# The cross-attention query projection of a hybrid decoder block, as a streamed Strassen step in place of dense 128x512 blocks

## The chip, the core and the metric

The kernel runs on one core of one Trainium2 chip, as one launch. The metric is the device time of the launch in microseconds (us), lower is better. Before the change three timed runs gave 1946.44, 1946.65 and 1947.6 us, a median of 1946.65 us.

## The reference

One decoder layer over 1024 tokens of width 1024 in float32: a mixer (an SSD branch and a gated-linear-attention branch, merged through gates), cross-attention over 256 memory tokens, and a SwiGLU feed-forward part, each behind an RMSNorm and with a residual add. What the change touches:

```python
merged = sigmoid(g_ssd) * (y_ssd @ w_up_ssd) + sigmoid(g_gla) * (y_gla @ w_up_gla)
h = h + merged @ w_o                                   # mixer's residual
n = rmsnorm(h, norm_xattn)
q = (n @ w_xq).reshape(B, S, 4, 256)                   # <- the query projection
k, v = split(rmsnorm(mem, norm_mem) @ w_xkv, 2)
p = softmax(einsum('bshd,bmhd->bhsm', q, k) * 256 ** -0.5)
h = h + einsum('bhsm,bmhd->bshd', p, v).reshape(B, S, D) @ w_xo
h = h + (silu(g) * u) @ w_ffn_out                      # g, u = split(rmsnorm(h, norm_ffn) @ w_ffn_in, 2)
```

## The kernel before

Activations lie with channels on the 128 partitions and 1024 tokens along the row. A float32 product is made of three products of rounded halves (type fp32r): a tile is split into a high part (ScalarE, `ACT`, a copy to fp32r) and a low part (VectorE, `DVE`, a subtraction), and TensorE (`PE`) adds high x high, high x low and low x high in PSUM. `split` (L226) issues such a pair.

The large projections use a Strassen scheme in Winograd's form: seven products of quarter matrices in place of eight, called B11, B21, T1, B22, T2, T3, T4 here, with sums of quarters prepared beforehand. Five projections do not: `dense` (L1236) runs `w_up_ssd`, `w_up_gla`, `w_o`, `w_xq` and `w_xo` as 16 blocks each (8 groups of 128 output channels by 2 halves of the tokens), 24 matmuls of 128x512 a block. The text calls the first three of them dense stages 0 to 2, `w_xq` the query stage. `Left` (L1190) streams their weights: 1 MB pieces `raw` (four buffers, `aux`), split into a ring of two tiles `wd`.

Dense stage 2 (`w_o`) ends each block in `residual` (L1357): DVE adds the block to a piece `ga` of the residual stream, the sum is stored (`h_d<-ga`), `put_xq` (L1365) makes the high and low parts of the query stage's input (`hl`), and `Stats.take` (L487) squares it on ACT into one buffer `sq` and adds that to `ssum`. Which of DVE and POOL adds is decided when the program is built, by `either` (L85).

Beside the dense stages runs `presum` (L1297): for each of 11 pieces of `w_ffn_out` it loads 1 MB into the one buffer `pre`, makes four sums on POOL (one into `sa`, three in place), and stores each of them (`down_d<-sa`, `down_d<-pre`). The next load waits until the stores have read the buffer. These sums are left operands of the last Strassen products, far behind. All transfers named here are issued by SP, in the order that a scheduler wrote when the program was built: every engine takes its instructions in order, and one that waits holds up those behind it.

`load_kv` (L1385) fetches one head's keys and values into two `ga` buffers and splits them into `kvhl`. The program calls it for the first head behind the query stage, but the scheduler may write it earlier. Then attention runs per head and half of the tokens (`Att`): scores, softmax, transposes, values; the blocks of `w_xo` (dense stage 4) are written between and behind them, and the feed-forward part follows.

SBUF is shared out in slots of 8 KB a partition: 14 `op`, 4 `aux`, 4 `m`. PSUM has 8 banks: 4 `acc`, 4 `bank`.

Of the kernel before, what the change touches and what calls it, by code (L numbers as in the profile page):

```python
# [27 lines left out]
KP = D_FF // 256  # L28
# [50 lines left out]
def block_kernel(ctx: ExitStack, tc: tile.TileContext, t: dict, out: bass.AP):  # L79
    nc = tc.nc  # L80
    now = [0.0]
    PE, ACT, SP = Tensor(nc.tensor, now), nc.scalar, nc.sync
    DVE, POOL = Meter(nc.vector, now, 0.06, 1.04e-3), Meter(nc.gpsimd, now, 0.08, 2.25e-3)
# [15 lines left out]
    def dram(name, *shape):  # L99
        return dr.tile(list(shape), F32, name=name, tag=name)  # L100
# [14 lines left out]
    yg_d = dram("yg_d", D, TOK)  # L115
    act_d = dram("act_d", 7 * D_FF // 2, HALF)
    down_d = dram("down_d", 4 * D_FF // 2, HALF)
    kT_d = dram("kT_d", D, MEM)
    vm_d = dram("vm_d", MEM, D)
    cs_d = dram("cs_d", P, P)  # L120
# [105 lines left out]
    def split(src, hi, lo, e=None):  # L226
        ACT.activation(hi, src, AF.Copy)  # L227
        sub(e or DVE, lo, src, hi)
# [5 lines left out]
    class Operands:  # L234
# [44 lines left out]
    class Unit:  # L279
# [267 lines left out]
    for k in range(NB):  # L547
        p = bank()
# [633 lines left out]
    def quad(src, base, i, j):  # L1182
        q = rp.tile([P, HALF], F32, name="ga", tag="ga")
        SP.dma_start(q, src[base + i * P:base + (i + 1) * P, half(j)])
        return q

    HOME = ("aux", "aux", "m", "m")
    JS = (0, 1)

    class Left:  # L1190

        def __init__(s, mats):
            s.seq, s.raw, s.w, s.ring = [(W, u) for W in mats for u in range(4)], [], [], []

        def load(s, n):
            while len(s.raw) < min(n, len(s.seq)):
                W, u = s.seq[len(s.raw)]
                r = slot("aux", (P, NB, 256), name="raw")  # L1200
                SP.dma_start(r, W[:, 256 * u:256 * u + 256].rearrange("(k p) c -> p k c", p=P))
                s.raw.append(r)

        def upto(s, n):
            while len(s.w) < min(n, 2 * len(s.seq)):
# [12 lines left out]
            s.upto(n + 2)  # L1218
            return s.w[n]

    left = Left((t["w_up_ssd"], t["w_up_gla"], t["w_o"], t["w_xq"], t["w_xo"]))

    def paired(keys):

        return [(lambda k=k: slot(k, (P, 2, TOK), F32R, name="hl")) for k in keys]

    def hl(slots_, k):
        if callable(slots_[k]):
            slots_[k] = slots_[k]()
        return slots_[k]  # L1230

    def into(slots_, k, j, src, e=None):
        x = hl(slots_, k)
        split(src, x[:, 0, half(j)], x[:, 1, half(j)], e)

    def dense(no, ins, post, pre=lambda o, j: None, js=JS):  # L1236

        todo = [(o, j) for o in range(NB) for j in (js if o + 1 < NB else js[::-1])]
        got = [pre(*x) for x in todo[:2]]
        for n, (o, j) in enumerate(todo):  # L1240
            w = left[NB * no + o]
# [12 lines left out]

    EVEN, ODD = ("op",) * 8, ("op",) * 6 + ("aux",) * 2
    i_ys, i_yg, i_wo, i_xq, i_q, i_xo = (paired(x) for x in (EVEN, ODD, EVEN, ODD, EVEN, EVEN))

    def fetch(src, dst, gain=None):

# [34 lines left out]
    sums["m"] = pool("sa2", 2, stack=st5)  # L1294
    s1 = Stats(rp)

    def presum():  # L1297


        r = slot("m", (P, 2, D), name="pre")  # L1300
        for k in range(KP):
            SP.dma_start(r, t["w_ffn_out"][256 * k:256 * k + 256, :].rearrange("(j p) c -> p j c", p=P))
# [3 lines left out]
            put = lambda n, ap: SP.dma_start(down_d[(n * KP + k) * P:(n * KP + k + 1) * P, :], ap)  # L1306
# [12 lines left out]

    def quad_of(src):  # L1320
        return lambda o, j: quad(src, o * P, 0, j)
# [35 lines left out]
    def residual(store, stats, gain, put, scale=1.0):  # L1357
        def post(o, j, p, q):
            DVE.scalar_tensor_tensor(q, p, scale, q, ALU.mult, ALU.add)
            SP.dma_start(store[o * P:(o + 1) * P, half(j)], q)  # L1360
            put(o, j, q, col(gain, o))
            stats.take(j, q)
        return post

    def put_xq(o, j, q, g):  # L1365
        x = hl(i_xq, o)
        h, l = x[:, 0, half(j)], x[:, 1, half(j)]
        ACT.activation(h, q, AF.Copy, scale=g)
        DVE.scalar_tensor_tensor(l, q, g, h, ALU.mult, ALU.subtract)

    def waiting(g, n):
        for _ in range(n):
            yield
        for _ in g:
            yield
# [6 lines left out]

    kv = []

    def load_kv(h):  # L1385
        es = [rp.tile([P, 2, 256], F32, name="ga", tag="ga") for _ in range(2)]
        h_ = slot("m" if h < 3 else "op", (P, 2, 4, 256), F32R, name="kvhl")
        SP.dma_start(es[0], kT_d[h * 256:(h + 1) * 256, :].rearrange("(i p) m -> p i m", p=P))
        SP.dma_start(es[1], vm_d[:, h * 256:(h + 1) * 256].rearrange("(i p) c -> p i c", p=P))
        for i in range(2):  # L1390
            split(es[i], h_[:, 0, 2 * i:2 * i + 2], h_[:, 1, 2 * i:2 * i + 2])
        kv.append(h_)

    xsc = cp.tile([P, NCH], F32, name="xsc")
# [12 lines left out]
    run(dense(3, i_xq, lambda o, j, p, g: into(i_q, o, j, p)), (xq_side(), 1.0), (early, 1.0))  # L1407
    drain(early)
    load_kv(0)
    u_xo_stats = Stats(rp)  # L1410

    class Att:
# [121 lines left out]
        ACT.activation(b_xo[o][:, half(j)], q, AF.Copy, scale=g)  # L1534

    B = Operands(b_xo, 4, order=("B11", "T1", "B21", "B22", "T2", "T3", "T4"))
    for n, _ in enumerate(dense(4, i_xo, residual(h2_d, u_xo_stats, "norm_ffn", put_xo), quad_of(h1_d), js=(1, 0))):
        if n >= 8:
            B.upto(n - 7)
        if n == 12:  # L1540
            gu[0][0].load()
        if n == 14:
            gu[0][1].load()
# [207 lines left out]
```

## Time and profile before

| what | us |
|---|---|
| median of three timed runs (1946.44 to 1947.6) | 1946.65 |
| the profiled execution: its span | 1949.0 |
| PE busy in it | 1916.2 |
| DVE, ACT, POOL busy | 1298.5, 845.8, 557.8 |
| mean granted TensorE clock | 0.998 |

The profiled execution has no time of its own beside its span; the span lies 2.35 us above the median. Times in the trace count from the span's start. In a line, `acc<-hl,wd` means that a tile `acc` is written from tiles `hl` and `wd`; `x16` counts instructions; what stands behind `<-` in brackets ended the idle time before it. A matmul row's duration reaches past the start of the next, so that rates are read from starts.

### The profile page before, as it was taken

How to read it: one execution, taken by the hardware profiler on the slowest of the kernel's cores; microseconds unless marked ns; L12 is line 12 of the kernel's file. 1: busy time of each engine (PE TensorE's matmuls, PEld its weight loads, DVE VectorE, ACT ScalarE, POOL GpSimd, SP SyncE). 2: the span in 40 equal slices, each digit the busy share in tenths (PEclk: the TensorE clock that was granted, in tenths of full speed). 3: DMA queues.
4: the chain of work that ended last, by engine and by line, in shares of the span. 5: the costliest groups of instructions: out<-in, count | busy, mean ns of one | idle time of the engine just before them, and what ended most of it. 6: DMA issues, size and time to landing. Idle time of an engine off the chain costs nothing.

```text
span 1949.0 us, 26264 instructions
## 1 busy us (share of the span) xinstructions
PE 1916.2 (98%) x9776; PEld 1615.6 (83%) x9776; DVE 1298.5 (67%) x1873; ACT 845.8 (43%) x1485; POOL 557.8 (29%) x428
## 2 busy tenths in 40 slices
PE   7999999999999999999999999999999999999998
PEld 7998787888878888788887888888888888888888
DVE  7766879877776764655534237677777777766566
ACT  7534564655553444643223235444333333345243
POOL 0012334345543231022433000006445544320002
PEclk9999999999999999999999999999999999999999
DMA  9423383446553653997675201442233224177463
GB/s 341 144 93 101 130 307 107 152 161 186 174 173 123 198 167 124 348 346 270 226 269 164 82 22 44 140 141 82 90 126 110 82 100 144 42 271 239 157 224 126
DMA packets 237875, 317.98 MB, mean 163 GB/s; under 512 B 16538, under 2 KB 156036, under 8 KB 237748
## 3 DMA queue, kind: packets, MB, share of 16 engines
q1 hardware_dynamic: 236020, 310.01, 47.4%
q10 hardware_dynamic: 1728, 6.29, 0.8%
q8 instruction: 77, 1.26, 0.3%
q14 instruction: 50, 0.41, 0.1%
HBM read 215.27 MB, written 100.99 MB: 162 GB/s over the span
## 4 chain that ended last, share of the span: by engine, by line
PE 43%; DMA 3%; POOL 2%; DVE 1%; issue 1%; ACT 1%; POOLq 0%; SPq 0%; DVEq 0%; ACTq 0%
PE acc L51 38%; PE bank L51 4%; DMA pre<-in_w_ffn_out_dram 1%; POOL pre L73 1%; DMA down_d<-pre 1%; PE bank L55 1%; POOL ssum L73 0%; DVE hl L73 0%; POOL sa L73 0%; DMA h_d<-ga 0%; DMA ga<-vm_d 0%; DVE wd L73 0%; ACT wd L227 0%; ACT sq L493 0%; DVE phl L73 0%
## 5 line engine op out<-in xcount | busy, mean ns | idle before, releaser
L51 PE MATMUL acc<-hl,wd 128*128 128x512 f32 x1920 | 440.4, 390 | 3.6 <-DVE wd L73 2.0
L51 PEld LDWEIGHTS acc<-hl,wd 128*128 128x128 f32 x1920 | 359.6, 188 | 80.7 <-DVE wd L73 3.3
L73 DVE TENSOR_TENSOR wlo<-raw,whi 128x512 fp32r<-128x512 f32 x272 | 236.4, 875 | 103.6 <-ACT whi L227 103.5
L227 ACT ACTIVATE whi<-raw 128x512 fp32r<-128x512 f32 x272 | 169.5, 629 | 247.6 <-PE acc L51 201.0
L73 DVE TENSOR_TENSOR o<-acc,o 128x512 f32<-128x512 f32 (+1 forms) x256 | 172.6, 676 | 108.8 <-PE acc L51 95.4
L51 PE MATMUL acc<-fs 128*128 128x512 f32 (+1 forms) x792 | 155.7, 356 | 0.1
L51 PEld LDWEIGHTS acc<-fs 128*128 128x128 f32 x792 | 130.7, 189 | 20.8 <-issue 0.5
L73 DVE TENSOR_TENSOR fs<-fr,fs 128x1024 fp32r<-128x1024 f32 (+1 forms) x84 | 98.9, 1217 | 36.5 <-ACT fs L227 36.4
L227 ACT ACTIVATE fs<-fr 128x1024 fp32r<-128x1024 f32 (+1 forms) x84 | 79.2, 982 | 95.9 <-PE acc L51 31.2
L73 POOL TENSOR_TENSOR raw<-raw,sa 128x512 f32<-128x512 f32 x44 | 57.1, 1297 | 207.8 <-DVE wlo L73 207.8
L73 POOL TENSOR_TENSOR sa<-raw 128x512 f32<-128x512 f32 x43 | 69.6, 1619 | 107.0 <-DMA raw<-in_w_in_dram 78.9
L227 ACT ACTIVATE whi<-sa 128x512 fp32r<-128x512 f32 x96 | 59.6, 626 | 93.7 <-PE acc L51 92.3
L73 DVE TENSOR_TENSOR wlo<-sa,whi 128x512 fp32r<-128x512 f32 x96 | 80.9, 843 | 13.7 <-ACT whi L227 12.7
L73 DVE TENSOR_TENSOR wd<-raw,wd 128x1024 fp32r<-128x1024 f32 x40 | 52.8, 1323 | 47.6 <-ACT wd L227 47.2
L73 POOL TENSOR_TENSOR rstd<-rstd,mhalf 128x4 f32<-128x4 f32 (+1 forms) x7 | 8.7, 1246 | 257.0 <-DVE rstd L73 257.0
L227 ACT ACTIVATE wd<-raw 128x1024 fp32r<-128x1024 f32 x40 | 42.2, 1057 | 90.4 <-PE acc L51 89.8
L51 PE MATMUL acc<-T4h,whi 128*128 128x512 f32 x192 | 76.3, 397 | 2.4 <-DVE o L73 2.4
L51 PE MATMUL acc<-B22h,wlo 128*128 128x512 f32 x192 | 75.7, 394 | 1.5 <-DVE wlo L73 1.5
L51 PE MATMUL acc<-T1h,whi 128*128 128x512 f32 x192 | 76.3, 397 | 0.0
L51 PE MATMUL acc<-T2h,whi 128*128 128x512 f32 x192 | 75.9, 395 | 0.0
L51 PE MATMUL acc<-T3h,whi 128*128 128x512 f32 x192 | 75.9, 395 | 0.0
L51 PE MATMUL acc<-B22h,whi 128*128 128x512 f32 x192 | 75.7, 394 | 0.0
(399 smaller groups left out, 4698.6 us busy)
## 6 DMA issues: line engine op xcount, KB each, us to landing
raw<-in_w_in_dram SPq DMA_DIRECT2D x26, 1024.0 KB, 5.9
raw<-in_w_ffn_in_dram SPq DMA_DIRECT2D x22, 1024.0 KB, 6.5
act_d<-o SPq DMA_DIRECT2D x77, 256.0 KB, 2.1
fr<-act_d SPq DMA_DIRECT2D x35, 512.0 KB, 7.9
pre<-in_w_ffn_out_dram SPq DMA_DIRECT2D x11, 1024.0 KB, 10.0
fr<-down_d SPq DMA_DIRECT2D x20, 512.0 KB, 3.9
down_d<-pre SPq DMA_DIRECT2D x33, 256.0 KB, 3.1
h_d<-ga SPq DMA_DIRECT2D x32, 256.0 KB, 3.1
```

The source lines that it names most:

```text
L51: return s.e.matmul(o, x, y, **kw)
L55: return s.e.transpose(o, x, i)
L73: return f(*a, **kw)
L227: ACT.activation(hi, src, AF.Copy)
```

## The change

The query stage leaves `dense` and becomes a class `Wide`: Strassen's seven products over all 1024 channels, each product 512 x 512 x 512, done in two steps of 24 matmuls for all four groups of 128 output rows. Its weights come as quarters of `w_xq` (B11, B21, T4) or as sums of quarters (T1, B22, T2, T3), and these sums are four new items at the front of `presum`, stored in a new DRAM buffer `xqs_d`. `put_xq` keeps its result whole in four quarter tiles `rq`; their differences and the splits into `ws` are made in the stage. The products B11, T2, T3 and T4 add up in the same four `acc` banks, T1 and B22 in four `bank` banks, B21 in four others; the parts are put together in tiles `wk` and split into the attention's operands `hl`. The first head's key/value splits are held in program order late in the stage (`kv_side`), and `w_xo`'s first two weight splits are called for at step 12 (`next_left`). `presum` is advanced faster in this stage (1.5 in place of 1.0 a step).

```diff
+    class Wide:
+        SEQ = ("B11", "T1", "B22", "T2", "B21", "T3", "T4")
+        LEFT = {"B11": (0, 0), "B21": (0, 1), "T1": 0, "B22": 3, "T2": 1, "T3": 2, "T4": (1, 1)}
+        COMB = {"T1": ((0, 0), (0, 1), (0, 0)), "T2": ((0, 0), (1, 1), (0, 0)), "T3": ((0, 1), (1, 1), (0, 1)),
+                "T4": ((1, 0), (1, 0), (0, 0))}
+        RIGHT = {"B11": (0, 0), "B22": (1, 1), "B21": (1, 0), "T1": (0, 0), "T2": (0, 0), "T3": (0, 1), "T4": (1, 0)}
+        OUT = {"B11": (0, 0), "T1": (1, 1), "B22": (0, 1), "T2": (0, 1), "B21": (0, 0), "T3": (1, 1), "T4": (1, 0)}
...
+        def load(s, n):
+            while len(s.raw) < min(n, 7):
+                src = s.LEFT[s.SEQ[len(s.raw)]]
+                if isinstance(src, tuple):
+                    i, j = src
+                    w = s.W[half(j), half(i)]
+                else:
+                    w = s.sums_d[half(src), :]
+                r = slot(s.keys[len(s.raw)], (P, 4, HALF), name="wr")
+                SP.dma_start(r, w.rearrange("(k p) c -> p k c", p=P))
+                s.raw.append(r)
...
+        def prep(s, n):
+            while len(s.ops) < min(n, 14):
+                m, kp = divmod(len(s.ops), 2)
+                s.load(m + 1)
+                name, c = s.SEQ[m], slice(2 * kp, 2 * kp + 2)
+                x = [slot("op", (P, 2, 2, HALF), F32R, name="ws") for _ in range(2)]
+                with ahead():
+                    if name in s.COMB:
+                        o, a, b = (s.quad(*ij)[:, c] for ij in s.COMB[name])
+                        sub(s.two(o), o, a, b)
+                    split(s.raw[m][:, c], x[0][:, 0], x[0][:, 1])
+                    split(s.quad(*s.RIGHT[name])[:, c], x[1][:, 0], x[1][:, 1])
+                s.ops.append(x)
+        def evac(s, name, u, p):
+            i, j = s.OUT[name]
+            o = p if name == "T4" and s.base is None else s.home(i, j)[:, u]
+            first = name in ("B11", "T1", "B22")
...
+                elif first:
+                    ACT.activation(o, p, AF.Copy)
+                elif name != "T4":
+                    add(DVE, o, p, o)
+                if not first:
+                    s.post(i, j, u, o)
+        def steps(s):
...
+                for kp in range(2):
+                    s.load(m + 3)
+                    s.prep(x + 3)
+                    w, b = s.ops[x]
+                    for u in range(4):
+                        for k in range(2):
+                            for n, (a, c) in enumerate(((0, 0), (0, 1), (1, 0))):
+                                PE.matmul(banks[u], w[:, a, k, u * P:(u + 1) * P], b[:, c, k],
...
-    left = Left((t["w_up_ssd"], t["w_up_gla"], t["w_o"], t["w_xq"], t["w_xo"]))
+    left = Left((t["w_up_ssd"], t["w_up_gla"], t["w_o"], t["w_xo"]))
...
+        todo = [(t[w].rearrange("(j k p) c -> k p j c", j=2, p=P)[k], d, 4, k) for w, d in wides for k in range(4)]
+        todo += [(t["w_ffn_out"][256 * k:256 * k + 256, :].rearrange("(j p) c -> p j c", p=P), down_d, KP, k)
+                 for k in range(KP)]
...
     def put_xq(o, j, q, g):
-        x = hl(i_xq, o)
-        h, l = x[:, 0, half(j)], x[:, 1, half(j)]
-        ACT.activation(h, q, AF.Copy, scale=g)
-        DVE.scalar_tensor_tensor(l, q, g, h, ALU.mult, ALU.subtract)
+        ACT.activation(xq.quad(o // 4, j)[:, o % 4], q, AF.Copy, scale=g)
...
+    def kv_side():
+        for _ in range(2):
+            yield
+        es = fetch_kv(0)
+        for _ in range(9):
+            yield
+        split_kv(es, pinned)
+        yield
+
+    def next_left():
+        left.limit = len(left.seq)
+        left.upto(26)
+        yield
+
-    run(dense(3, i_xq, lambda o, j, p, g: into(i_q, o, j, p)), (xq_side(), 1.0), (early, 1.0))
+    run(xq.steps(), (xq_side(), 1.0), (early, 1.5), (kv_side(), 1.0), (waiting(next_left(), 12), 1.0))
     drain(early)
-    load_kv(0)
...
-    for n, _ in enumerate(dense(4, i_xo, residual(h2_d, u_xo_stats, "norm_ffn", put_xo), quad_of(h1_d), js=(1, 0))):
+    for n, _ in enumerate(dense(3, i_xo, residual(h2_d, u_xo_stats, "norm_ffn", put_xo), quad_of(h1_d), js=(1, 0))):
```

More of the change, by code (lines that the diff above doesn't have):

```diff
@@ L117, in block_kernel @@
     down_d = dram("down_d", 4 * D_FF // 2, HALF)
+    xqs_d = dram("xqs_d", 2 * D, HALF)
     kT_d = dram("kT_d", D, MEM)
@@ L1188, in block_kernel, with __init__, quad, home @@
     JS = (0, 1)
+    class Wide:
[5 more added lines that the diff above has]
+        OUT = {"B11": (0, 0), "T1": (1, 1), "B22": (0, 1), "T2": (0, 1), "B21": (0, 0), "T3": (1, 1), "T4": (1, 0)}
+        def __init__(s, W, sums_d, post, keys, side, base=None, scale=1.0, two=None):
+            s.W, s.sums_d, s.post, s.keys, s.side, s.base, s.scale = W, sums_d, post, keys, side, base, scale
+            s.two = two or (lambda ap: DVE)
+            s.q, s.raw, s.ops, s.keep, s.chain = {}, [], [], {}, None
+        def quad(s, i, j):
+            if (i, j) not in s.q:
+                s.q[i, j] = slot("op", (P, 4, HALF), name="rq")
+            return s.q[i, j]
+        def load(s, n):
[9 more added lines that the diff above has]
+                s.raw.append(r)
+        def home(s, i, j):
+            if (i, j) not in s.keep:
+                k = s.keep[i, j] = slot(s.side[len(s.keep)], (P, 4, HALF), name="wk")
+                if s.base is not None:
+                    SP.dma_start(k, s.base[half(i), half(j)].rearrange("(u p) c -> p u c", p=P))
+            return s.keep[i, j]
+        def prep(s, n):
[15 more added lines that the diff above has]
+            first = name in ("B11", "T1", "B22")
+            with ahead():
+                if s.base is not None:
+                    DVE.scalar_tensor_tensor(o, p, s.scale, o, ALU.mult, ALU.add)
+                elif first:
[5 more added lines that the diff above has]
+        def steps(s):
+            x = 0
+            for m, name in enumerate(s.SEQ):
+                if name in ("B11", "T1", "B21"):
+                    banks = [(acc if name == "B11" else bank)() for _ in range(4)]
+                    if name == "B11":
+                        s.chain = banks
+                elif name in ("T2", "T3", "T4"):
+                    banks = s.chain
+                fresh = name in ("B11", "T1", "B21")
+                if s.base is not None:
+                    s.home(*s.OUT[name])
+                for kp in range(2):
[6 more added lines that the diff above has]
+                                PE.matmul(banks[u], w[:, a, k, u * P:(u + 1) * P], b[:, c, k],
+                                          start=fresh and kp + k + n == 0, stop=kp + k == 2 and n == 2,
+                                          skip_group_check=True)
+                    x += 1
+                    if kp:
+                        for u in range(4):
+                            s.evac(name, u, banks[u])
+                    yield
@@ L1195, in __init__ @@
             s.seq, s.raw, s.w, s.ring = [(W, u) for W in mats for u in range(4)], [], [], []
+            s.limit = 12
         def load(s, n):
-            while len(s.raw) < min(n, len(s.seq)):
+            while len(s.raw) < min(n, s.limit):
                 W, u = s.seq[len(s.raw)]
@@ L1204, in upto @@
         def upto(s, n):
-            while len(s.w) < min(n, 2 * len(s.seq)):
+            while len(s.w) < min(n, 2 * s.limit):
                 u, i = divmod(len(s.w), 2)
@@ L1255, in block_kernel @@
     EVEN, ODD = ("op",) * 8, ("op",) * 6 + ("aux",) * 2
-    i_ys, i_yg, i_wo, i_xq, i_q, i_xo = (paired(x) for x in (EVEN, ODD, EVEN, ODD, EVEN, EVEN))
+    i_ys, i_yg, i_wo, i_q, i_xo = (paired(x) for x in (EVEN, ODD, EVEN, EVEN, EVEN))
     def fetch(src, dst, gain=None):
@@ L1295, in block_kernel @@
     s1 = Stats(rp)
+    wides = (("w_xq", xqs_d), )
     def presum():
         r = slot("m", (P, 2, D), name="pre")
-        for k in range(KP):
-            SP.dma_start(r, t["w_ffn_out"][256 * k:256 * k + 256, :].rearrange("(j p) c -> p j c", p=P))
+        todo = [(t[w].rearrange("(j k p) c -> k p j c", j=2, p=P)[k], d, 4, k) for w, d in wides for k in range(4)]
+        todo += [(t["w_ffn_out"][256 * k:256 * k + 256, :].rearrange("(j p) c -> p j c", p=P), down_d, KP, k)
+                 for k in range(KP)]
+        for src, dst, kn, k in todo:
+            SP.dma_start(r, src)
             yield
@@ L1305, in presum @@
             s1_ = sums["m"].tile([P, HALF], F32, name="sa", tag="sa", bufs=2)
-            put = lambda n, ap: SP.dma_start(down_d[(n * KP + k) * P:(n * KP + k + 1) * P, :], ap)
+            put = lambda n, ap: SP.dma_start(dst[(n * kn + k) * P:(n * kn + k + 1) * P, :], ap)
             add(POOL, s1_, a(1, 0), a(1, 1))
@@ L1363, in residual @@
         return post
+    xq = Wide(t["w_xq"], xqs_d, lambda i, j, u, p: into(i_q, 4 * i + u, j, p), ("aux", "op", "aux") * 3, ("aux",) * 3)
     def put_xq(o, j, q, g):
-        x = hl(i_xq, o)
-        h, l = x[:, 0, half(j)], x[:, 1, half(j)]
-        ACT.activation(h, q, AF.Copy, scale=g)
-        DVE.scalar_tensor_tensor(l, q, g, h, ALU.mult, ALU.subtract)
+        ACT.activation(xq.quad(o // 4, j)[:, o % 4], q, AF.Copy, scale=g)
     def waiting(g, n):
@@ L1383, in block_kernel, with fetch_kv, split_kv, load_kv @@
     kv = []
-    def load_kv(h):
+    def fetch_kv(h):
         es = [rp.tile([P, 2, 256], F32, name="ga", tag="ga") for _ in range(2)]
-        h_ = slot("m" if h < 3 else "op", (P, 2, 4, 256), F32R, name="kvhl")
         SP.dma_start(es[0], kT_d[h * 256:(h + 1) * 256, :].rearrange("(i p) m -> p i m", p=P))
         SP.dma_start(es[1], vm_d[:, h * 256:(h + 1) * 256].rearrange("(i p) c -> p i c", p=P))
+        return es
+    def split_kv(es, pin=lambda x: x):
+        h_ = slot("m" if len(kv) < 3 else "op", (P, 2, 4, 256), F32R, name="kvhl")
         for i in range(2):
-            split(es[i], h_[:, 0, 2 * i:2 * i + 2], h_[:, 1, 2 * i:2 * i + 2])
+            pin(ACT.activation(h_[:, 0, 2 * i:2 * i + 2], es[i], AF.Copy))
+            pin(sub(DVE, h_[:, 1, 2 * i:2 * i + 2], es[i], h_[:, 0, 2 * i:2 * i + 2]))
         kv.append(h_)
+    def load_kv(h):
+        split_kv(fetch_kv(h))
     xsc = cp.tile([P, NCH], F32, name="xsc")
@@ L1405, in xq_side @@
         yield
-    run(dense(3, i_xq, lambda o, j, p, g: into(i_q, o, j, p)), (xq_side(), 1.0), (early, 1.0))
+    def kv_side():
[9 more added lines that the diff above has]
+        left.upto(26)
+        yield
+    run(xq.steps(), (xq_side(), 1.0), (early, 1.5), (kv_side(), 1.0), (waiting(next_left(), 12), 1.0))
     drain(early)
-    load_kv(0)
     u_xo_stats = Stats(rp)
```

## The prediction

> **What bounds the kernel now.** First the page's head, then busy time by stretch for the stretches around the query stage.
>
> ```profile
> span 1949.0 us, 26264 instructions
> PE 1916.2 (98%) x9776; PEld 1615.6 (83%) x9776; DVE 1298.5 (67%) x1873; ACT 845.8 (43%) x1485; POOL 557.8 (29%) x428
> core 0: us, PE busy (x) PEld busy (x) DVE busy (x) ACT busy (x) POOL busy (x), PEclk, DMA share, GB/s
> 977.00:1069.00 92.00, 89.93 (x394) 73.20 (x393) 40.27 (x44) 28.04 (x41) 33.06 (x25) 1.00 0.65 217
> 1069.00:1156.50 87.50, 87.35 (x394) 72.27 (x392) 23.56 (x30) 20.50 (x30) 4.81 (x4) 1.00 0.20 63
> 1156.50:1220.00 63.50, 63.11 (x398) 55.94 (x397) 45.69 (x117) 38.18 (x101) 0.00 (x0) 1.00 0.10 34
> ```
>
> TensorE is the bound, in the query stage (second stretch) wholly: DVE, ACT, POOL and the DMA rest there. So fewer matmuls are worth their time, as long as nothing else becomes late. PE's timeline gives the rate and the waits.
>
> ```profile
> 804.50 226.96 PE L51 MATMUL acc<-hl,wd 128*128 128x512 f32 x1000 [0.43 <-DVE wd L73]
> 1031.84 0.73 PE L51 MATMUL acc<-hl,wd 128*128 128x512 f32 x2 [0.38 <-ACT wd L227]
> 1033.34 21.60 PE L51 MATMUL acc<-hl,wd 128*128 128x512 f32 x94 [0.76 <-DVE wd L73]
> 1055.09 0.73 PE L51 MATMUL acc<-hl,wd 128*128 128x512 f32 x2
> 1056.60 17.97 PE L51 MATMUL acc<-hl,wd 128*128 128x512 f32 x78 [0.78 <-DVE wd L73]
> 1156.50 7.96 PE L51 MATMUL acc<-kvhl,hl 128*128 128x256 f32 x65
> ```
>
> A thousand matmuls in 226.96 us: 0.227 us each. Eight stand ahead of 804.50, so the 1152 of the first three dense stages would end at 804.5 + 1144 x 0.2269 = 1064.1 without the later waits; counted on from 1056.60 they end at 1067.0. Stage 2 loses 2.9 us. The query stage runs from 1067.0 to 1156.5, 89.5 us.
>
> Who is late there: ACT, whose split of `wd` stands behind something else.
>
> ```profile
> 1028.18 0.63 ACT L493 ACTIVATE sq<-ga 128x512 f32<-128x512 f32 x1 [11.71 <-POOL ssum L73]
> 1030.75 1.04 ACT L227 ACTIVATE wd<-raw 128x1024 fp32r<-128x1024 f32 x1
> 1053.45 0.63 ACT L227 ACTIVATE kvhl<-ga 128x512 fp32r<-128x512 f32 x1 [10.52 <-DMA ga<-kT_d]
> 1053.99 1.04 ACT L227 ACTIVATE wd<-raw 128x1024 fp32r<-128x1024 f32 x1
> ```
>
> At 1028 the one `sq` buffer waits for POOL, which adds `ssum` only behind the presums; at 1053 a key/value split waits for its load.
>
> **The change part by part.** *Fewer matmuls.* The stage's matmuls in PE's order, before:
>
> ```order
> L51 MATMUL acc<-hl,wd 128x512
> L51 MATMUL bank<-ones,ssum 128x1
> L51 MATMUL acc<-hl,wd 128x512 x305
> L51 MATMUL acc<-kvhl,hl 128x256 x65
> L55 MATMUL bank<-ident,pe 128x128 x2
> ```
>
> and now, with `ws` for the new operands:
>
> ```order
> L51 MATMUL acc<-ws 128x512 x21
> L51 MATMUL bank<-ws 128x512 x4
> L51 MATMUL acc<-ws 128x512 x27
> L51 MATMUL bank<-ws 128x512 x44
> L51 MATMUL acc<-ws 128x512 x4
> L51 MATMUL bank<-ws 128x512 x48
> L51 MATMUL acc<-ws 128x512 x11
> L51 MATMUL bank<-ones,ssum 128x1 x8
> ```
>
> 384 become 7 x 48 = 336: 48 x 0.227 = **10.9 us** less. And four matmuls of T2 (`acc<-ws x4`) now stand ahead of B22's 48, behind 96 of B11 and T1. From 1064.1 PE is there at 1064.1 + 96 x 0.227 = **1085.9**.
>
> *Waits of stage 2.* In ACT's order before:
>
> ```order
> L227 ACTIVATE kvhl<-ga 128x512
> L227 ACTIVATE wd<-raw 128x1024
> L1368 ACTIVATE hl<-ga,cols 128x512
> L493 ACTIVATE sq<-ga 128x512
> L227 ACTIVATE kvhl<-ga 128x512 x3
> ```
>
> and now, in the query stage at T2's weights, with `wk` the product's copy out of PSUM:
>
> ```order
> L228 ACTIVATE ws<-rq 128x1024
> L1254 ACTIVATE wk<-acc 128x512 x2
> L228 ACTIVATE ws<-wr 128x1024
> L228 ACTIVATE ws<-rq 128x1024
> L228 ACTIVATE ws<-wr 128x1024
> L1254 ACTIVATE wk<-bank 128x512
> ```
>
> The key/value splits have left stage 2, and POOL's order has no `ssum` add there any more (DVE makes them): both causes above go, up to 2.9 us. What waits for a load now is the `ws<-wr` behind `wk<-acc x2`: T2's first weight split, with the copies of T1's banks queued behind it, which B22 needs.
>
> *The longer presum.* Four more items go through one buffer. SP's order at the last presum item, before:
>
> ```order
> L1306 DMA down_d<-sa 128x512
> L1360 DMA h_d<-ga 128x512
> L1306 DMA down_d<-pre 128x512 x3
> L1184 DMA ga<-xT_d 128x512
> L1360 DMA h_d<-ga 128x512
> ```
>
> and now:
>
> ```order
> L1406 DMA pre<-in_w_ffn_out_dram 128x2x1024
> L1490 DMA ga<-kT_d 128x2x256
> L1464 DMA h_d<-ga 128x512
> L1410 DMA down_d<-sa 128x512
> L1491 DMA ga<-vm_d 128x2x256
> L1410 DMA down_d<-pre 128x512 x2
> L1464 DMA h_d<-ga 128x512
> L1410 DMA down_d<-pre 128x512
> L1490 DMA ga<-kT_d 128x2x256
> L1464 DMA h_d<-ga 128x512
> L1491 DMA ga<-vm_d 128x2x256
> L1222 DMA wr<-xqs_d 128x4x512
> ```
>
> The last row is T2's weights. SP issues them only when the fifteenth item is stored and a `ga` buffer is free again. Eleven items stand where they stood (the first four are now the query weights' sums), four more follow. Their pace, from POOL's timeline (an item's first sum, and the end of item 11):
>
> ```profile
> 941.90 1.28 POOL L73 TENSOR_TENSOR sa<-pre 128x512 f32<-128x512 f32 x1 [8.39 <-issue]
> 956.87 2.16 POOL L73 TENSOR_TENSOR sa<-pre 128x512 f32<-128x512 f32 x1 [8.56 <-issue]
> 971.21 1.29 POOL L73 TENSOR_TENSOR sa<-pre 128x512 f32<-128x512 f32 x1 [7.53 <-DMA pre<-in_w_ffn_out_dram]
> 984.92 1.29 POOL L73 TENSOR_TENSOR sa<-pre 128x512 f32<-128x512 f32 x1 [7.76 <-DMA pre<-in_w_ffn_out_dram]
> 1005.81 1.28 POOL L73 TENSOR_TENSOR sa<-pre 128x512 f32<-128x512 f32 x1 [14.29 <-DMA h_d<-ga]
> 1021.77 1.28 POOL L73 TENSOR_TENSOR sa<-pre 128x512 f32<-128x512 f32 x1 [7.53 <-DMA pre<-in_w_ffn_out_dram]
> 1024.37 2.53 POOL L73 TENSOR_TENSOR pre<-pre 128x512 f32<-128x512 f32 x2
> ```
>
> And single parts of an item, from the chain of waits (a store until it has landed, a load until it has landed):
>
> ```profile
> 963.70 2.17 DMA down_d<-pre
> 977.18 2.66 DMA down_d<-pre
> 979.91 4.84 DMA pre<-in_w_ffn_out_dram
> 991.54 4.95 DMA down_d<-pre
> 1015.47 6.15 DMA pre<-in_w_ffn_out_dram
> ```
>
> Item 11 ends at 1024.37 + 2.53 = 1026.9. Items came 15.0, 14.3 and 13.7 us apart, then 20.9 and 16.0 where three weight loads shared the DMA. I take 13.7 (few loads are left) and once 2.0 for T1's load beside it (the store at 991.54 beside such loads took 4.95 in place of 2.66): 4 x 13.7 + 2 = 56.8, item 15 ends at 1083.7.
>
> ```profile
> raw<-in_w_in_dram SPq DMA_DIRECT2D x26, 1024.0 KB, 5.9
> h_d<-ga SPq DMA_DIRECT2D x32, 256.0 KB, 3.1
> L227 ACT ACTIVATE wd<-raw x40: 1039/1061/1065, 800.8 to 1275.2; 128x1024 fp32r<-128x1024 f32 x40
> L73 DVE TENSOR_TENSOR wd<-raw,wd x40: 1211/1225/2319, 803.2 to 1276.3; 128x1024 fp32r<-128x1024 f32 x40
> ```
>
> The rest of the way goes by these durations, in turn. The store of block 14, issued 0.9 before that end, lands (3.1); the load of `kT_d` into its buffer and the store of block 15 are issued (0.8); that store lands (3.1), which frees the buffer for `vm_d`; two issues (0.7): 1083.7 - 0.9 + 7.7 = 1090.5. T2's 1 MB lands 5.9 later, ACT splits weights and right operand (2 x 1.06): **1098.5**. PE waits 1098.5 - 1085.9 = **12.6 us**.
>
> *After the wait* 240 matmuls remain, 54.5 us. B22's first bank is free 0.8 late: ACT makes one more split (1.06) and the copy (0.63, as the key/value copy of that size above), less the four matmuls. The statistics' one-column matmuls are 16 in the trace; eight such took 0.81 elsewhere on PE's timeline, so 1.6:
>
> ```profile
> 1305.18 0.95 PE L51 MATMUL bank<-ones,ssum 128*128 128x1 f32 x8
> 1305.99 0.49 PE L51 MATMUL acc<-T1h,whi 128*128 128x512 f32 x1
> ```
>
> Sum: 1098.5 + 56.9 = **1155.4**, against 1156.5: -1.1 us. The end hangs on the chain of presums alone: a stage 2 that gains less only shortens the wait.
>
> *DVE in the stage.* The row for half-size splits:
>
> ```profile
> L73 DVE TENSOR_TENSOR hl<-acc,hl x16: 679/686/692, 1076.1 to 1159.3; 128x512 fp32r<-128x512 f32 x16
> ```
>
> 28 splits and 8 differences of 1024 a row are 36 x 1.225 = 44.1, 12 additions, 16 splits into `hl` and four into `kvhl` 32 x 0.69 = 22.0, two of `wd` 2.5: 68.6 us in a stage that lasts 91 with the wait. The matmuls, with the wait in them, are the cover; without the wait 76 us of matmuls would leave 7. ACT has less: 28 x 1.06 and some 32 x 0.6, 49 us. The other edits I cost at nothing: `w_xo`'s first loads stand behind T4's on SP, and attention's 64 us cover them; the first head's keys are split before the last product is out.
>
> *Attention* keeps its matmuls in another order; PE idled 0.4 of 63.5 us there. I take nothing, and -0.4 to +2 as bounds. Feed-forward keeps PE's order.
>
> **The rivals.** *The wait is short or absent (faster).* With the shortest parts (POOL 5.1 an item as from 1021.77 to 1026.9, store 2.17, load 4.84, 0.2 between) items come 12.3 us apart, T2 is ready at 1089.9 and the stage ends at 1146.8: -9.7. With no wait at all 1064.1 + 336 x 0.227 + 1.6 = 1142.0: -14.5. For it: no weight loads but T1's stand among the last four items on SP. Against it: no two items came closer than 13.7. More than 3.9 us is won below 13.0 an item.
>
> *POOL slows beside DVE (slower).* Items 14 and 15 now fall beside DVE's densest stretch. The `wd` subtraction ranges from 1.21 to 2.32 us, the POOL sum from 1.28 to 2.16. At 16.0 us an item (the last interval) with a 6.15 load T2 is ready at about 1106, the end at 1163: +6.5. It decides above 15.0 an item. Against it: DVE stands idle once PE waits.
>
> *PE restarts at half speed.* At the program's start the timeline shows 128x256 matmuls 0.21 us apart, later 0.12:
>
> ```profile
> 12.63 0.41 PE L51 MATMUL acc<-wlo,mh 128*128 128x256 f32 x1
> 12.84 0.42 PE L51 MATMUL acc<-whi,ml 128*128 128x256 f32 x1
> 15.32 0.28 PE L51 MATMUL acc<-whi,ml 128*128 128x256 f32 x1
> 15.44 0.28 PE L51 MATMUL acc<-whi,mh 128*128 128x256 f32 x1
> ```
>
> Four us at that rate cost 1.8, and the forecast would be +0.7. PE's longest wait for DVE is 1.7 us (below), so no row shows whether 12 us bring it back.
>
> ```profile
> PE acc L51 <- DVE wlo L73: 3.7, 7, 1.7
> ```
> The Trainium skill (TensorE: Matmul & The Clock Gate, Part 1) says they do: about 3.4 us without work halve the clock, and as long a busy stretch restores it. By it the price is an estimate of 1.7 us.
>
> *The change not doing what it says* is ruled out by the order above.
>
> **How the numbers follow.** The sum is made within the profiled span of 1949.0, 2.35 us above the median; the difference is set on the median: 1946.65 - 1.1 = **1945.5**. A measurement can tell 0.2%, 3.9 us. The forecast, with or without the half-speed start (even odds, 1945.5 or 1947.3), has 0.40; the short wait 0.37; slow presums 0.23. The range takes the shortest chain, 1937, and the longest with a half-speed start, 1946.65 + 6.5 + 1.8, rounded to 1954; the wait that is absent (1932) stays outside. Faster 0.37, same 0.40, slower 0.23.
>
> **What would show it.** 336 matmuls `acc`/`bank<-ws`, no PE wait in stage 2; one long PE wait ahead of the four T2 matmuls, released by ACT `ws`, and ACT's idle before it ended by the DMA `wr<-xqs_d`, itself issued behind the last `down_d<-pre`. If that load lands ahead of 1084, the forecast is wrong to the good; if a DVE `ws` ends PE's waits, DVE became the bound.

## The result, and the profile after

The changed kernel takes 1964.93 us (median of four runs, 1959.67 to 1968.29) against 1947.12 (four runs, 1946.44 to 1950.22): a ratio of 1.0084, 95% interval 1.0063 to 1.0104. It is slower by 0.84%, where -1.1 us had been forecast. Its profiled execution took 1968.0 us, the span is 1966.3, so 17.3 above the span of before. Two of the four runs took 1968.0 and 1968.3 us, the other two 1959.7 and 1961.9; the profile is of a longer one, and what is shorter in the others no trace shows. First the head of its page, then busy time by stretch.

```profile
span 1966.3 us, 26289 instructions
PE 1907.1 (97%) x9728; PEld 1608.1 (82%) x9728; DVE 1335.5 (68%) x1911; ACT 872.2 (44%) x1517; POOL 570.8 (29%) x430
```

```profile
core 0: us, PE busy (x) PEld busy (x) DVE busy (x) ACT busy (x) POOL busy (x), PEclk, DMA share, GB/s
1062.00:1084.00 22.00, 22.00 (x99) 18.17 (x97) 18.13 (x17) 11.00 (x14) 14.79 (x4) 1.00 0.32 102
1084.00:1111.00 27.00, 0.33 (x2) 0.00 (x0) 0.34 (x1) 1.43 (x2) 6.09 (x5) 0.59 0.75 260
1111.00:1114.00 3.00, 2.38 (x6) 1.90 (x7) 3.00 (x3) 3.00 (x5) 0.00 (x0) 0.50 0.10 38
1114.00:1126.00 12.00, 12.00 (x50) 9.80 (x49) 8.44 (x8) 7.04 (x11) 0.00 (x0) 0.91 0.28 89
```

PE has 48 matmuls fewer and is busy 9 us less, but from 1084 to 1111 hardly anything runs except POOL and the DMA. PE's timeline shows the one wait, and the slow start behind it:

```profile
1062.41 4.92 PE L51 MATMUL acc<-ws 128*128 128x512 f32 x21
1074.19 10.13 PE L51 MATMUL bank<-ws 128*128 128x512 f32 x44
1111.62 2.07 PE L51 MATMUL acc<-ws 128*128 128x512 f32 x4 [27.29 <-ACT ws L228]
1113.49 12.31 PE L51 MATMUL bank<-ws 128*128 128x512 f32 x48
1125.64 2.65 PE L51 MATMUL acc<-ws 128*128 128x512 f32 x11
1137.46 11.04 PE L51 MATMUL bank<-ws 128*128 128x512 f32 x48
1148.34 21.92 PE L51 MATMUL acc<-ws 128*128 128x512 f32 x96
1170.10 7.12 PE L51 MATMUL acc<-kvhl,hl 128*128 128x256 f32 x58
```

It stands where the forecast put it, ahead of the four matmuls of T2, but is 27.3 us long and not 12.6. The 52 matmuls behind it take 14.02 us (1111.62 to 1125.64) in place of 52 x 0.227 = 11.8; the granted clock there is 0.50, then 0.91. ACT's timeline and SP's show what the wait hangs on, the load of T2's weights behind the last stores of presum:

```profile
1075.12 1.08 ACT L1254 ACTIVATE wk<-acc 128x512 f32<-128x512 f32 x2
1109.57 1.06 ACT L228 ACTIVATE ws<-wr 128x1024 fp32r<-128x1024 f32 x1 [33.37 <-DMA wr<-xqs_d]
```

```profile
1097.82 0.32 SPq L1410 DMA_DIRECT2D down_d<-pre  x1
1099.62 0.37 SPq L1490 DMA_DIRECT2D ga<-kT_d  x1
1100.03 0.47 SPq L1464 DMA_DIRECT2D h_d<-ga  x1
1103.22 0.37 SPq L1491 DMA_DIRECT2D ga<-vm_d  x1
1103.63 0.47 SPq L1222 DMA_DIRECT2D wr<-xqs_d  x1
```

So the chain is the forecast one, in the forecast order. What was late is the presum in it. POOL's timeline has the end of item 11, then the first sums of items 12 to 15 and the end of the last:

```profile
1022.71 3.00 POOL L73 TENSOR_TENSOR pre<-pre 128x512 f32<-128x512 f32 x2
1035.39 1.30 POOL L73 TENSOR_TENSOR sa<-pre 128x512 f32<-128x512 f32 x1 [9.68 <-issue]
1048.53 1.61 POOL L73 TENSOR_TENSOR sa<-pre 128x512 f32<-128x512 f32 x1 [7.53 <-DMA pre<-in_w_ffn_out_dram]
1069.13 12.16 POOL L73 TENSOR_TENSOR sa<-pre 128x512 f32<-128x512 f32 x1 [15.12 <-DMA pre<-in_w_ffn_out_dram]
1092.75 1.26 POOL L73 TENSOR_TENSOR sa<-pre 128x512 f32<-128x512 f32 x1 [7.62 <-DMA pre<-in_w_ffn_out_dram]
1095.31 2.48 POOL L73 TENSOR_TENSOR pre<-pre 128x512 f32<-128x512 f32 x2
```

One sum took 12.16 us where its like take 1.3. DVE's timeline just then: instructions back to back, without an idle mark, from 1058.94 to 1078.92 + 1.22 = 1080.14. These are the first and the last of them, and the next one, 30 us later.

```profile
1058.94 1.23 DVE L73 TENSOR_TENSOR ws<-rq,ws 128x1024 fp32r<-128x1024 f32 x1 [1.08 <-ACT ws L228]
1078.92 1.22 DVE L73 TENSOR_TENSOR ws<-rq,ws 128x1024 fp32r<-128x1024 f32 x1
1110.65 1.23 DVE L73 TENSOR_TENSOR ws<-wr,ws 128x1024 fp32r<-128x1024 f32 x1 [30.52 <-ACT ws L228]
```

The sum ends at 1081.29, 1.15 us behind DVE's last. PE was still at work then; its long wait begins at 1084.3. The chain of waits shows the other slow piece: item 13's store took 8.44 us (B22's 1 MB load was issued 0.5 ahead of it, the nearest cause in the trace), where item 14's took 2.01.

```profile
1054.15 8.44 DMA down_d<-pre
1062.60 6.36 DMA pre<-in_w_ffn_out_dram
1069.13 12.15 POOL sa L73
1085.15 2.01 DMA down_d<-pre
```

Last, attention and w_xo run from 1170.10 to 1314.29, 144.2 us in place of 140.5. Part of that shows as two waits of transposes for VectorE's splits:

```profile
1187.46 0.66 PE L55 MATMUL bank<-ident,pe 128*128 128x128 f32 x4 [1.22 <-DVE hl L73]
1188.86 0.66 PE L55 MATMUL bank<-ident,pe 128*128 128x128 f32 x4 [0.75 <-DVE hl L73]
```

### The profile page after: what moved, and what is told of

Its sections match the earlier page's. It is cut to its first block, busy times and chain, and to the rows that moved or that the text cites. A ratio compares the mean times of both kernels' runs of the same rounds, so it can differ in the third digit from the quotient of the medians.

```text
span 1966.3 us, 26289 instructions
## 1 busy us (share of the span) xinstructions
PE 1907.1 (97%) x9728; PEld 1608.1 (82%) x9728; DVE 1335.5 (68%) x1911; ACT 872.2 (44%) x1517; POOL 570.8 (29%) x430
## 5 line engine op out<-in xcount | busy, mean ns | idle before, releaser
L51 PE MATMUL acc<-hl,wd 128*128 128x512 f32 x1536 | 350.8, 390 | 1.7 <-ACT wd L228 1.3
L51 PEld LDWEIGHTS acc<-hl,wd 128*128 128x128 f32 x1536 | 287.6, 188 | 63.1 <-ACT wd L228 2.5
L73 POOL TENSOR_TENSOR sa<-pre 128x512 f32<-128x512 f32 x15 | 30.6, 2041 | 213.5 <-DMA pre<-in_w_xq_dram 93.2
L51 PE MATMUL acc<-T2l,whi 128*128 128x512 f32 x192 | 75.1, 391 | 0.0
```

The source lines that it names most:

```text
L51: return s.e.matmul(o, x, y, **kw)
L73: return f(*a, **kw)
```

## Theory and rivals

The theory was: T2 is late because its load stands on SP behind a presum that four items have made longer and one starved sum longer still; with that gone the stage gains what its 48 matmuls are worth. The rivals: VectorE bounds the new stage, so that its `ws` splits take the place of the wait; the DMA is short, wherever the load stands; the late key/value splits make the attention longer. The changed kernel's own trace speaks against the second: T2's load, issued at 1103.63, took 5.91 us to land (1109.54), the 5.9 that were forecast.

## The experiments

Ratios are to the kernel before on the same chip, with 95% intervals. "Stage" is from the first `acc<-ws` to the first `acc<-kvhl,hl`, "attention" from there to feed-forward's first matmul.

**The presum's tail left out.** The diff skips loads and sums of the last three items and keeps their stores (the expectation says seven; three it is).

```diff
         for src, dst, kn, k in todo:
+            put = lambda n, ap: SP.dma_start(dst[(n * kn + k) * P:(n * kn + k + 1) * P, :], ap)
+            if k > 7:
+                for n in range(4):
+                    put(n, r[:, n // 2, half(n % 2)])
+                continue
             SP.dma_start(r, src)
```

> The last seven presum items (from the ninth on) are neither loaded nor summed; only their stores are issued, so the feed-forward product works on wrong sums. Theory: the presum chain of loads, POOL sums and stores is what SP stands in; without it T2's load is issued as soon as its buffer is free, no PE wait above 2 us in the query stage, ratio about 0.994, as with the loads on another queue. If the attention still takes 144 us against 140.5, its loss belongs to its own order and not to the wait ahead of it; if it takes 141, the wait made it. Rival, VectorE bounds the stage: waits for DVE's ws of 8 to 15 us, ratio about 1.000.

Measured: 1942.14 against 1945.7, ratio 0.9983 (0.9974 to 0.9992); stage 84.1 us, attention 144.1.

```profile
1085.92 2.08 PE L51 MATMUL acc<-ws 128*128 128x512 f32 x4 [3.08 <-ACT ws L228]
1087.79 12.97 PE L51 MATMUL bank<-ws 128*128 128x512 f32 x48
```

The wait falls from 27.3 to 3.1 us and no wait for VectorE takes its place: the chain it is (this edit takes the three loads' traffic away as well). But the gain is a quarter of the expected: 3.1 us of wait are left, and a restart at half speed again, 2.9 us (the 52 matmuls take 14.67 us where 11.8 are due). The attention's 3.6 us, which the expected ratio allows for, come without the long wait too.

**The low parts on ScalarE.** `split(...)` of both `ws` operands becomes two ScalarE copies, so that VectorE does not subtract there (the low parts hold wrong values).

> The low part of each ws operand is a second copy on ScalarE in place of VectorE's subtraction with two SBUF inputs, so the low parts hold the wrong values; SP's order around the stage is otherwise as in the changed kernel. Theory: POOL's presum sum of 12.2 us at 1069 is VectorE's doing, whose subtractions ran without a gap there; with those gone the sum takes 1.3 to 2.5 us, T2's load is issued about 11 us earlier and PE waits about 16 us instead of 27. Rival, the sum is slow because of the transfers beside it (a 1 MB load and stores): it stays above 8 us and the wait stays at 25 to 28 us.

Measured, one run: 1955.66. POOL's timeline for item 14, and PE's wait:

```profile
1066.13 1.29 POOL L73 TENSOR_TENSOR sa<-pre 128x512 f32<-128x512 f32 x1 [13.87 <-DMA pre<-in_w_ffn_out_dram]
```

```profile
1099.17 7.69 PE L51 MATMUL acc<-ws 128*128 128x512 f32 x24 [16.59 <-ACT ws L1243]
```

Both as the theory has it: 1.29 us and a wait of 16.6, which is 10.7 less, as the sum is 10.9 shorter. VectorE's unbroken run had starved the sum.

**All weight loads on ScalarE's queue; the last four on it.** `SP.dma_start(r, ...)` in `Wide.load` becomes `ACT.dma_start`, first for all seven, then from T2 on.

> The seven weight loads of the query stage are issued by ScalarE's queue instead of SyncE's; nothing else is edited. Theory: T2's weights are late only because their load stands behind the last presum items in SP's order. Then the 27.3 us wait ahead of T2's four matmuls falls below 2 us, the half-speed restart (about 2 us) goes with it, the query stage takes 336 x 0.227 + 1.6 = 78 us, and the ratio to the kernel before is about 0.994 (the attention still 3.7 us longer). Rival, VectorE bounds the stage: the wait for the load goes, but matmul waits for DVE's ws of 8 to 15 us in sum take its place, and the ratio is 0.999 to 1.003. Rival, the DMA is what is short: the load is issued early but takes over 15 us beside the presum, T2 still waits 5 to 10 us, ratio 0.997 to 1.000.

> Only the four weight loads from T2 on go to ScalarE's queue; those of B11, T1 and B22 stay on SyncE's, since with all seven there ScalarE had stood 4.8 us in stage 2 and 3.9 us in T1. Theory: the place on SP's queue was the cause of the wait at T2, and it alone. The stage starts at 1062, takes 336 x 0.227 + 1.8 = 78 us without a PE wait above 1 us, the attention 144.2; the ratio to the kernel before is 0.995 to 0.997. POOL's sum beside VectorE's dense stretch still takes over 10 us, and nobody waits for it. Rival, the loads on ScalarE's queue hold up its splits again: PE waits of 4 to 8 us for ACT's or DVE's ws, ratio 0.998 to 1.000.

Measured: 1.0045 (1.0031 to 1.0059) and 1.0029 (1.0019 to 1.0039). Both beat the changed kernel. T2's four matmuls themselves hardly wait any more (no wait marked with all seven loads there, 0.73 us with four), but the waiting moves ahead of them. With all seven, PE waited 4.8 us late in stage 2 for ScalarE's `wd` and 3.9 us among T1's matmuls. With four, it waited 13.4 us among T1's: ScalarE's queue's timeline shows T2's load held until a key/value load had landed, which SP issues between the presum's stores, and every split behind it held as well (the last row is PE's):

```profile
1090.95 0.38 ACTq L1222 DMA_DIRECT2D wr<-xqs_d  x1
1091.37 1.06 ACT L228 ACTIVATE ws<-rq 128x1024 fp32r<-128x1024 f32 x1 [21.16 <-DMA ga<-vm_d]
```

```profile
1092.48 7.29 PE L51 MATMUL bank<-ws 128*128 128x512 f32 x24 [13.39 <-ACT ws L228]
```

The built program says why: T2's load waits for two of the eight semaphores that count transfers, and one is waited for at the count which that `vm_d` load reaches. It shares no data with T2's weights. Another queue did not take the load out of SP's line, and my expectation was wrong: what ScalarE has behind the load now waits with it. The same run shows the starving again. POOL's sum started at 1068.56, VectorE's run ended at 1071.17 + 2.35 = 1073.52, the sum at 1074.66, 1.14 behind it:

```profile
1068.56 6.10 POOL L73 TENSOR_TENSOR sa<-pre 128x512 f32<-128x512 f32 x1 [13.95 <-DMA ga<-kT_d]
```

```profile
1071.17 2.35 DVE L73 TENSOR_TENSOR rq<-rq 128x1024 f32<-128x1024 f32 x2
```

**Each load one product earlier.** `s.load(m + 3)` becomes `s.load(m + 4)`.

> Each quarter's weight load is called one product earlier, which puts T2's load ahead of the last three presum loads on SP; B21's, T3's and T4's still stand behind the last presum item. Theory: T2 no longer waits; the next load behind the presum, B21's, is late instead: issued at about 1104, landed at 1110, split by 1112, where PE is there at 1084 + 2 x 48 x 0.227 = 1106, so a wait of 4 to 8 us. The ratio is about 0.997. Rival, VectorE bounds the stage: waits for DVE's ws from T2 on, ratio 1.000 or above.

Measured: 1.0069 (1.0048 to 1.0091). T2 no longer waits; the wait is one product on, as expected, but 18.6 us long and not 4 to 8, since POOL's sum was starved for 15.6 us this time (VectorE had more splits to run without a gap, until 1084.33, and the sum ended 1.15 behind that):

```profile
1069.87 15.61 POOL L73 TENSOR_TENSOR sa<-pre 128x512 f32<-128x512 f32 x1 [14.44 <-DMA pre<-in_w_ffn_out_dram]
```

```profile
1112.46 1.06 ACT L228 ACTIVATE ws<-wr 128x1024 fp32r<-128x1024 f32 x1 [27.85 <-DMA wr<-in_w_xq_dram]
```

```profile
1116.89 3.57 PE L51 MATMUL bank<-ones,ssum 128*128 128x1 f32 x16 [18.64 <-ACT wk L1254]
```

**Keys not held late.** To the kernel with four loads on ScalarE: without `kv_side`, with `load_kv(0)` behind the stage as before.

> As the kernel with the last four loads by ScalarE, but the first head's keys and values are fetched and split by a call behind the stage, as in the kernel before, and not held in program order. Theory: holding the splits late costs nothing and saves ScalarE's wait for their load in stage 2 (1.5 us in the kernel before at 1055); without the hold 0 to 2 us come back, ratio within 0.001 of the kernel with the hold. Rival: the late splits are what makes the attention 3.7 us longer; without the hold it takes 141 us and the ratio falls by 0.002.

Measured: 1.0071 (1.0057 to 1.0085), attention still 144.1. ScalarE stands 25.3 us on the key load, and the stage begins late:

```profile
1067.65 0.63 ACT L1497 ACTIVATE kvhl<-ga 128x512 fp32r<-128x512 f32 x1 [25.34 <-DMA ga<-kT_d]
```

```profile
1078.73 13.92 PE L51 MATMUL acc<-ws 128*128 128x512 f32 x48 [16.67 <-ACT ws L228]
```

I had expected no difference. Holding the splits is worth 0.4% here, and is not what lengthens the attention.

**The kernel before, with 15 items.** Its presum gets the four items of the query weights in front, which nobody reads; the query stage is the old one.

> The kernel before with the four sums of the query weights added in front of its presum; nobody reads them. Theory: the longer presum by itself costs little, since nothing that PE needs soon stands behind it on SP; ratio 0.999 to 1.002, at most the stage-2 waits for POOL and for the key/value load grow by 1 or 2 us. Rival: 8 MB more traffic and 16 more POOL sums cost time wherever they stand (contention with the weight loads and VectorE), ratio 1.003 to 1.006, the longer of which would be half of the change's loss.

Measured: 1.0109 (1.0096 to 1.0122), attention 140.5. This is the largest miss: I had it at 1.002 at most, and my rival at 1.006. Without any Strassen step the four items cost more than the whole change. From the first dense matmul to the attention it takes 18.8 us longer than before. PE's marked waits there add up to 14.1 us in place of 2.1, and what is left of the 18.8 are matmuls behind these waits, at a granted clock of 0.50 (25 of them in 8.65 us, where 5.7 are due). Two of the waits, 2.17 and 3.35 us, are for ScalarE's `wd`. It stands once behind a square that waits for POOL's `ssum`, and once behind the first head's splits, which wait for their loads on SP: the causes that the new stage does away with. The longest wait is new. ScalarE's second head waits for presum's last store, because its `kvhl` takes the buffer of `pre`, and the old stage's `hl` stands behind it (ScalarE's row, then PE's).

```profile
1085.95 1.15 ACT L228 ACTIVATE kvhl<-ga 128x512 fp32r<-128x512 f32 x2 [5.20 <-DMA down_d<-pre]
```

```profile
1088.71 12.36 PE L51 MATMUL acc<-hl,wd 128*128 128x512 f32 x45 [6.75 <-ACT hl L1372]
```

**The presum in half items.** Each item goes as two halves of 256 columns that alternate in the buffer, so that one half is loaded beside the other's sums; with T2's load early, with it as in the changed kernel, and in the kernel before as a control.

```diff
-        r = slot("m", (P, 2, D), name="pre")
+        r = slot("m", (P, 2, 2, 2, 256), name="pre")
...
+            for h in range(2):
+                for j in range(2):
+                    SP.dma_start(r[:, h, j], src[h, j])
...
+                a = lambda i, j: r[:, h, j, i]
```

> The presum runs in half items of 256 columns that alternate between two halves of its buffer, so that the load of one half goes beside the sums and stores of the other; T2's load is called one product earlier as in the run of that name. All work is done. Theory: the changed kernel's loss is the serial presum chain, whose last items hold T2's weights and the pre buffer. With the chain done before stage 2 ends there is no PE wait above 1 us in the query stage, which takes 78 us from about 1061; with an attention of 144.2 the span is about 1935 and the ratio 0.994 to 0.996. Rival, the stage is bound by VectorE or by the order of ScalarE's splits: waits of 4 to 8 us stay, ratio 0.998 to 1.000. Rival, the shorter pieces (1 KB runs, twice the transfers) make the presum slower than before: T2 waits, ratio above 1.000.

> The same presum in halves, with T2's load called where the changed kernel calls it, behind the key loads and the last residual stores on SP. Theory: as in the run without the last sums, the load comes some 2 us too late, PE waits about 3 us at T2 and four matmuls run at half speed; ratio 0.997 to 0.999. Rival: as above.

> The kernel before with its eleven presum items in halves; no Strassen step. A control: if the presum in halves gained by itself, it would show here. Theory: only stage 2's waits can go, 0 to 2.9 us, ratio 0.9985 to 1.0005. Rival, the presum holds up more than the waits show: ratio 0.995 to 0.997, and the gain of the two kernels above is not the Strassen step's.

Measured: 0.9995 (0.9986 to 1.0003), 1.0045 (1.0029 to 1.0061) and, for the control, 1.0021 (1.0010 to 1.0032). In the first the presum ends at 1071.4 instead of 1097.8, T2 does not wait, and the time is that of the kernel before: the loss is undone, and no gain is left. PE's timeline shows new waits ahead of the stage's first matmuls and among them; VectorE's row shows what the second is, a piece of the residual stream that comes late. SP's rows have its load: it was issued behind a presum's load and a presum's store, for which SP had stood 2.8 and 1.5 us, and landed 3.2 us later.

```profile
1066.51 0.73 PE L51 MATMUL acc<-ws 128*128 128x512 f32 x2 [2.46 <-ACT ws L228]
1069.48 0.80 PE L51 MATMUL acc<-ws 128*128 128x512 f32 x1 [2.23 <-DVE ga L73]
```

```profile
1068.73 0.69 DVE L73 SCALAR_TENSOR_TENSOR ga<-acc,ga 128x512 f32<-128x512 f32 x1 [2.49 <-DMA ga<-xT_d]
```

```profile
1062.89 0.54 SPq L1408 DMA_DIRECT2D pre<-in_w_ffn_out_dram  x1
1064.92 0.33 SPq L1412 DMA_DIRECT2D down_d<-sa  x1
1065.52 0.33 SPq L1185 DMA_DIRECT2D ga<-xT_d  x1
```

So here too something else stands behind the presum on SP. From the first dense matmul to feed-forward this run takes 492.5 us against 495.1 before: the waits, the slow start behind them and the attention's 3.6 us take most of what 48 matmuls and stage 2's waits would have given.

In the second, T2 waited 9.1 us, three times what I expected, and the stage's first matmuls waited 3.3 us for such a piece. The control was slower than the kernel before, so halves gain nothing by themselves.

**The attention's 3.7 us.** Three runs change only its order, by priorities: first scores first (`with ahead(): a.score(0)`) on the kernel with four loads on ScalarE, value and transpose splits first on the kernel with half items, and both edits on the kernel before.

> As the run before, and the first scores of each pair in the attention get the priority that splits have, which writes another order of the attention. Theory: the 3.7 us that attention and w_xo take longer in every kernel with the new stage (144.2 against 140.5) belong to the order that was written there, VectorE's above all, and not to the wait; in another order they take 139 to 146 us, the time follows by that, and with 140.5 the ratio is about 0.994. Rival: the 3.7 us come from what the stage leaves behind (late splits of the last product, keys and values split late); then it stays 144 us in any order.

> As the first of these, and in the attention the splits of the values and of the transposed weights get priority, which changes the order there again. Theory: the 3.7 us are waits of the transposes for VectorE's splits of the values; with those splits first the attention takes 141 to 143 us and the ratio is 0.001 to 0.0015 lower. Rival: they come from what the query stage leaves to do; it stays at 143.5 to 144.5.

> The kernel before, with the first scores of each pair in the attention given the priority that splits have: another order of the attention, and no new query stage. If the order of the attention is what costs 3.0 to 3.7 us with the new stage, another order behind the old stage can cost as much: attention and w_xo take 142 to 145 us against 140.5. If what the new stage leaves behind is the cause, the old stage gives 140 to 141 us in this order too.

> The kernel before, with the splits of the values and of the transposed weights given priority, as in the last run with the new stage, where the attention took 143.9 us. By the order 142 to 145 us; by what the new stage leaves behind 140 to 141 us.

Measured: 1.0030 (1.0019 to 1.0041) and 0.9993 (0.9982 to 1.0004); 1945.35 and 1948.31 in one run each against 1946.06. The attention takes 143.5 (from the stage's last matmul, with the twelve scores added that now stand ahead of it) and 143.9 us behind the new stage in these orders, 141.4 (23 matmuls of the query stage that fell into it taken off) and 140.6 behind the old one. So my theory that the order costs it is not borne out: behind the old stage three orders give 140.5 to 141.4, behind the new one three give 143.5 to 144.2 (145.5 in the run with all loads on ScalarE's queue). What is left is that the new stage leaves something to do that costs 2 to 4 us; that is argued, not shown, and what it is, is not settled. No version was measurably faster than the kernel before with all work done.

## Where the prediction held and where it failed

The measured 1964.93 us lies 11 above the upper end of the range, 1954. Step by step:

- *48 matmuls fewer at 0.227 us, 10.9 us*: held (48 in 10.88, 1137.46 to 1148.34 on PE's timeline).
- *The waits of stage 2 go*: held. From the first dense matmul, 1.46 us earlier in this profile than before, the stage begins 261.9 us later; the forecast has 262.2.
- *PE waits at T2 for the load that stands behind the fifteenth item, 12.6 us*: the place, the engine and the chain held, the size failed. Item 11 ended at 1025.7, or 1027.2 with the 1.46 added: 1026.9 forecast. The way from the last sum to T2 took 13.8 us (1097.79 to 1111.62) against 14.8.
- *Four items at 13.7 and once 2.0, 56.8 us*: this is the step that failed. They took 72.1 (1025.71 to 1097.79). 10.9 of the 15.3 are the starved sum (12.16 - 1.30); the other 4.4 are mostly item 13's store, for which I allowed 2.0 beside T1's load, where B22's load stood beside it and it took about 6 longer.
- *POOL slows beside DVE*: it was named as the rival that ends slower, and is what happened, but its price was wrong. I took the ranges of the rows of before, up to 2.16 us a sum and 16.0 an item, and called POOL safe because VectorE rests once PE waits. Here the sum did not get slower beside a run of such subtractions: it got nothing until the run ended, and this run lasted 11 us from the sum's start, all of it before PE's wait. My own count of VectorE's work in the stage, 68.6 us of 91, should have led me there. The Trainium skill (SBUF — State Buffer, Who interferes with whom) says that a VectorE instruction with two SBUF inputs and a GpSimd instruction that reads SBUF contend, and that one blocks fully. The traces agree: the sums ended 1.14 and 1.15 us behind VectorE's last instruction, and the run without those subtractions has 1.29 us.
- *Half speed after the wait*, +1.8, given even odds: it came, and cost 2.2 us (14.02 - 11.8, at a granted clock of 0.50).
- *Attention: nothing, -0.4 to +2*: failed, +3.7. The order had changed visibly; I had no row for what that costs, and the bound was a guess too narrow. What costs it stays open.

Together, from the forecast span of 1947.9: +14.6 for T2's readiness (0.3 + 15.3 - 1.0), +1.6 behind it, +3.7 in the attention, -1.5 for the earlier start (the runs shown here differ by up to 3.6 us in it): 1966.3. The starved sum, 10.9, is the largest single piece.

The run with 15 items shows what the prediction never asked: what a longer presum costs by itself. It treated the four items as a delay to one load only. Whatever is late on SP or takes the `pre` buffer pays, T2's weights here, the keys there. Its 1.0109 can't be read as a share of the changed kernel's loss, since its waits are others.

## What to carry to other kernels

A product saved on the bounding engine costs work on the others; price the helper chain that feeds it (one buffer, one queue, one engine) to its very end before counting the saving, and try the helper alone in the old kernel: that one run (1.0109) would have warned of a loss, if not of this one. Where GpSimd has a link in the chain, look for the stretch where VectorE runs without a gap, and take the link as starting when that stretch ends.

## What the runs showed of the hardware

- A GpSimd sum that meets VectorE's subtractions back to back waits for the first gap, over many instructions: 12.16 us in the changed kernel, 15.61 with each load one product earlier, 6.10 with the last four on ScalarE's queue, 8.25 with the first scores first. Where they alternate, VectorE pays instead: with all loads on ScalarE's queue POOL's sum took 1.78 us, and VectorE's subtractions 2.31 each in place of 1.22. No run here shows what decides between the two.
- 3.1 us without a matmul (the presum's tail left out) were enough for the next four to start 0.47 us apart (1085.92 to 1087.79), at a granted clock of 0.50. Less is enough too: in the run with value splits first PE waited 2.25 and then 0.88 us with one matmul between, and from 1069 to 1071 the granted clock was 0.50.
- A transfer on another engine's queue can still wait for SP's line, when the program lets both count on one semaphore: ScalarE stood 21.2 us here.
